# Lo parts of w_up by accumulating transfers in a two-layer hybrid encoder trunk

## The chip, the cores and the metric

The kernel runs on one core of one Trainium2 chip. The metric is the device time of one execution in microseconds. Other cores of the chip do no work of this kernel.

## The reference

The reference is a trunk of two layers over 256 tokens of width 2048, in float32. Each layer normalises the residual, projects it once, runs three groups of attention heads on the result, projects their concatenation back into the residual, and then applies an MLP with a squared ReLU:

```python
for l in range(DEPTH):                       # DEPTH = 2
    h = rmsnorm(x, norm_mix[l])
    proj = jnp.einsum('bsd,de->bse', h, w_in[l])          # 2048 x 3840
    ...                                                   # attention groups A, B, C
    x = x + jnp.einsum('bse,ed->bsd', mix, w_o[l])        # 2048 x 2048
    h = rmsnorm(x, norm_mlp[l])
    u = jax.nn.relu(jnp.einsum('bsd,df->bsf', h, w_up[l]))    # 2048 x 8192
    x = x + jnp.einsum('bsf,fd->bsd', u * u, w_down[l])       # 8192 x 2048
return rmsnorm(x, norm_final)
```

The change concerns the product with `w_up`, half of the MLP in each layer.

## The kernel before

**Two parts of a float32.** Every dense product is made on TensorE in three passes over operands of type fp32r. A weight tile W and an operand H are each split into a hi part, which is the value rounded to fp32r, and a lo part, which is the remainder W - hi. The three passes are hi·hi, hi·lo and lo·hi. Activations are split where they are made; weights are split as they arrive from memory.

**Steps.** The dense work is a list of 696 steps. A step takes one weight tile of 512 KB (128 partitions of 4 KB) and issues 24 matmuls with 256 columns (`w_up`, lines 611 to 613), or 12 with 512 columns (the other products, lines 446 to 448; one chunk of `w_in` has 24 of 256). A layer has 60 steps for `w_in`, 32 for `w_o`, and then the MLP in eight groups g: `up_steps(g)` has 16 steps (two chunks of 8), `down_steps(g)` has 16. They are listed as up(0), up(1), down(0), up(2), down(1), and so on to up(7), down(6), down(7). So in each layer the up steps come as one run of 32 and then six runs of 16, with 16 down steps between two runs; there are 128 up steps in a layer and 256 in all.

**Loading and splitting.** `load(i)` issues one transfer from the queue of SP into a tile `wraw` (six buffers). `split(i)` casts the tile to `whi` on ScalarE (line 783) and subtracts on VectorE to get `wlo` (line 784); `whi` and `wlo` have four buffers each. The loop over steps at the end issues loads up to 7 steps ahead (`LOOK_LOAD`) and splits up to 2 steps ahead (`LOOK_SPLIT`) of the step whose matmuls are written next. After each step `tick()` may add one piece of other work (attention, transposes). A scheduler then orders the instructions of each engine; each engine runs its own list in order.

**End of a chunk of w_up.** After the eighth step of a chunk, ScalarE applies ReLU to each of two PSUM banks (line 617), GpSimd squares the result in place (line 618), ScalarE casts it to hi (line 621) and VectorE subtracts for lo (line 622). These squares are all that GpSimd does in the up and down steps, except for the final norm.

Of the kernel before, what the change touches and what calls it, by code (L numbers as in the profile page):

```python
"""Hybrid encoder trunk (three attention groups, squared-ReLU MLP) on one core.

Dense products run on the tensor engine as float32 split exactly into two fp32r
parts (hi + lo); hi*hi + hi*lo + lo*hi carries float32's accuracy in three passes.
The residual stream, attention and normalisations stay on chip; only weights stream.
"""
# [27 lines left out]
OUT_ORDER = "ACB"  # L34
# mixer feature blocks of 256 (two k-blocks each): A 0-1, B 2-3, C 4-7
GROUP_BLOCKS = {"A": (0, 1), "B": (2, 3), "C": (4, 5, 6, 7)}
# [7 lines left out]
def tile_trunk(ctx: ExitStack, tc: tile.TileContext, x_in, w_in, w_o, w_up, w_down,  # L44
               gains, rowp, t5, rpb, gfin, cst, onehot, out):
    nc = tc.nc
    LOOK_LOAD, LOOK_SPLIT, BUDGET = 7, 2, 2.2
    N_WARM = 6
# [29 lines left out]

# [1 line left out]
    ident = cp.tile([P, P], F32, name="ident")  # L80
# [25 lines left out]
    def setup_tables():  # L106
        """Rope tables with the gains folded in: out = x * ctab + swap16(x) * stab."""
        nc.vector.tensor_scalar(negsink, rp[:, :, 0:8], -1.0, None, op0=ALU.mult)
        for l in range(L):
            nc.vector.tensor_scalar(rp[:, l, 8:72], rp[:, l, 8:72], 0.125, None, op0=ALU.mult)  # L110
            for which, off in (("q", 8), ("k", 72)):
                g = rp[:, l:l + 1, off:off + 64]
                c = cp.tile([P, NT, 64], F32, name=f"ctab_{which}{l}")
                s = cp.tile([P, NT, 64], F32, name=f"stab_{which}{l}")
                nc.vector.tensor_mul(c, cos_t, g.to_broadcast([P, NT, 64]))
                for a in range(4):
                    b = a ^ 1
                    nc.vector.tensor_mul(s[:, :, 16 * a:16 * a + 16], sin_t[:, :, 16 * a:16 * a + 16],
                                         g[:, :, 16 * b:16 * b + 16].to_broadcast([P, NT, 16]))
                ctab[which, l], stab[which, l] = c, s  # L120

    def setup_avec():
        """Relative-position vector of group A, reversed: avec[h, i] = bias(h, rel = 255 - i)."""
        t5x = cp.tile([33, 8], F32, name="t5x")
        nc.vector.memset(t5x[32:33, :], NEG)
        nc.sync.dma_start(t5x[0:32, :], t5)
        oh = dp.tile([33, 512], F32, tag="mid", bufs=6, name="oh")
        nc.sync.dma_start(oh, onehot)
        avs = dp.tile([8, 512], F32, tag="mid", bufs=6, name="avs")

        def mm():
            avp = tr_bank()
            nc.tensor.matmul(avp[0:8, :], t5x, oh, start=True, stop=True)
            nc.vector.tensor_copy(avs, avp[0:8, :])
            nc.sync.dma_start(avec, avs)
        add(mm, cost=0.9, delay=15.0)

# [1 line left out]
    bgq = []  # L139
# [7 lines left out]
    def add(fn, cost, after=(), delay=0):  # L147
        """Queue fn, `cost` us of PE time; it may start `delay` us from now or after the pieces in `after`."""
        p = Piece()
        p.fn, p.cost, p.after, p.delay, p.at, p.done = fn, cost, after, delay, cur[0], None  # L150
        bgq.append(p)
        return p
# [23 lines left out]

# [1 line left out]
    def hprep(key, gcol, j, hT, ss, done, fin_rs, late=0):  # L178
        """Column chunk j of x: partial sums of squares; k-blocks 4j..4j+3 of the operand."""
        def sq():  # L180
# [56 lines left out]

# [1 line left out]
    def q_transposes(src, pr0, qT):  # L239
        """src [P, t, heads*64]; 4 heads from pair pr0 -> qT [hi;lo, 4, 256]."""  # L240
        ps = tr_bank()
        psv = ps.rearrange("p (k t c) -> p k t c", k=2, t=NT)
        for pr in range(2):
            for t in range(NT):
                nc.tensor.transpose(psv[:, pr, t, :], src[:, t, (pr0 + pr) * P:(pr0 + pr + 1) * P], ident)  # L245
        psr = ps.rearrange("p (k c) -> p k c", k=2)
        for par in range(2):
            lo, hi = 64 * par, 64 * par + 64
            nc.scalar.copy(qT[0:64, par::2, :], psr[lo:hi, :, :])
        for par in range(2):  # L250
            lo, hi = 64 * par, 64 * par + 64
            nc.vector.tensor_sub(qT[64:128, par::2, :], psr[lo:hi, :, :], f(qT[0:64, par::2, :]))  # L252

    def k_transposes(src, pr0, npr, kh, kl):
        """src [P, t, heads*64]; head pairs pr0.. -> hi/lo [every head in both halves, heads, 256]."""
        ps = tr_bank()
        psv = ps.rearrange("p (k t c) -> p k t c", k=2, t=NT)
        for pr in range(npr):
            for t in range(NT):
                nc.tensor.transpose(psv[:, pr, t, :], src[:, t, (pr0 + pr) * P:(pr0 + pr + 1) * P], ident)  # L260
        psr = ps.rearrange("p (k c) -> p k c", k=2)[:, 0:npr, :]
        parts = [(slice(64 * half, 64 * half + 64), psr[64 * par:64 * par + 64], par)
                 for par in range(2) for half in range(2)]
        for rows, z, par in parts:
            nc.scalar.copy(kh[rows, par::2, :], z)
        for rows, z, par in parts:
            nc.vector.tensor_sub(kl[rows, par::2, :], z, f(kh[rows, par::2, :]))

    def v_split(ps, parts, t, r):
        """Value columns of one bank, scaled, as hi/lo; parts: (first column, heads, tile)."""  # L270
        src = [ps[:, c0:c0 + nh * 64].rearrange("p (h d) -> p h d", h=nh) for c0, nh, _ in parts]
# [6 lines left out]
    def rope(raw, H, which, l, outs):  # L278
        """raw [P, t, H, 64]: per-head RMS norm, gain and axial rotary, in place of outs(t)."""
        n = NT * H  # L280
# [21 lines left out]

# [1 line left out]
    class Unit:  # L304
# [4 lines left out]
    def queue_unit(u, *preps):  # L309
        """Scores, transposes of the weights, product with the values; spaced for the softmax between."""  # L310
        after = list(preps) + last_s[-1:]
# [86 lines left out]
    def mix_prep(l, grp, blk, raw, mixT, sqacc, done):  # L398
        """A finished block of 256 features: gained hi/lo operand and sum of squares."""
        m = big(F32R, 2, 2, 256)  # L400
# [30 lines left out]

# [1 line left out]
    steps = []  # L433

    class Step:
        def __init__(self, src, kk, n, pre, mm):
            self.src, self.kk, self.n, self.pre, self.mm = src, kk, n, pre, mm

    def mode_b(banks, h_tile, wh, wl, sub, first, last, n=512, blocks=(0, 1)):
        """out[tok, n] += operand^T W over the tile's k-blocks."""  # L440
        for t in blocks:
# [10 lines left out]
    def layer_steps(l):  # L452
# [10 lines left out]

        # -- input projection --
        def proj_evac(name, banks):
# [93 lines left out]

        # -- output projection --  # L560
        st["hT2"], st["ss2"] = [None] * 8, small(8)
# [26 lines left out]

        # -- MLP --
        uT = {}  # L590

        def up_steps(g):
            for c in range(2):
                fc = 2 * g + c
                box = {}
                for k in range(8):
# [3 lines left out]
                    def mm(wh, wl, k=k, fc=fc, box=box):  # L600
# [13 lines left out]
                        if k == 7:  # L614
                            for b in range(2):
# [7 lines left out]
                                uT[2 * fc + b] = u  # L623
                    steps.append(Step(w_up[l, fc * 8 + k], 2, 512, pre, mm))

# [48 lines left out]
    def final_chunk(j):  # L674
        """Squares of a finished column chunk; the final gain goes in ahead of the scale."""
        if not fin:
# [14 lines left out]
    def final_block(t):  # L691
        """Last chunk of token block t: norm over the whole row, scale, store."""
        square(3, t)
# [12 lines left out]

# [1 line left out]
    def bias_a(kv):  # L708
# [57 lines left out]

# [1 line left out]
    raw_t, hi_t, lo_t = {}, {}, {}  # L768

    def load(i):  # L770
        s = steps[i]
        w = wp.tile([P, s.kk, s.n], F32, tag="wraw", bufs=6, name=nm("wraw"))
        nc.sync.dma_start(w, s.src.rearrange("p (k n) -> p k n", k=s.kk))
        raw_t[i] = w

    def split(i):
        s = steps[i]
        w = raw_t.pop(i)
        h = wp.tile([P, s.kk, s.n], F32R, tag="whi", bufs=4, name=nm("whi"))
        lo = wp.tile([P, s.kk, s.n], F32R, tag="wlo", bufs=4, name=nm("wlo"))  # L780
        for part in ([slice(0, 1), slice(1, 2)] if i < 1 else [slice(0, s.kk)]):
            with tc.issue_after(h_act[-1]) if i < 2 else nullcontext():
                last_hi[0] = nc.scalar.copy(h[:, part], w[:, part]).ins  # L783
            nc.vector.tensor_sub(lo[:, part], w[:, part], f(h[:, part]))  # L784
        hi_t[i], lo_t[i] = h, lo

# [92 lines left out]
def _pack(w, nk):  # L879
    """[K, n] -> tiles [K/(128 nk), 128, nk*n]."""  # L880
    K, n = w.shape
# [61 lines left out]
```

## Time and profile before

| what | value |
|---|---|
| median of the two timed runs | 2089.51 us (2088.35 to 2090.66) |
| span of the profiled execution, first to last instruction | 2088.3 us |
| mean granted TensorE clock | 0.997 |
| TensorE busy with matmuls | 2066.0 us, 99% of the span |
| VectorE busy | 1273.8 us, 61% |
| ScalarE busy | 1041.4 us, 50% |
| GpSimd busy | 340.1 us, 16% |
| read from device memory | 377.34 MB |

The profiled execution has no time of its own beside its span; the lower of the two timed runs, 2088.35 us, is that span to within 0.1 us, so nothing measurable lies around it. "Busy" means that the engine had at least one instruction under way; matmuls overlap, so the busy time of TensorE doesn't say at what rate it worked. PE is TensorE's matmuls, PEld its weight loads, DVE VectorE, ACT ScalarE, POOL GpSimd and SP the engine that issues the loads. A window "A:B" is a stretch of the span in microseconds from its start.

### The profile page before, as it was taken

What the parts mean: (1) busy time and instruction counts of PE and PEld (TensorE: products, weight loads), DVE (VectorE), ACT (ScalarE), POOL (GpSimd) and SP (SyncE); (2) the same over time, 40 slices, a digit from 0 to 9 for tenths busy, and PEclk for the clock granted to TensorE, in tenths of its full rate; (3) what the DMA queues carried; (4) which work ended last, traced back from release to release, by engine and by line L of the source; (5) the groups of instructions that cost most, each with busy time, mean ns of one, the idle gap of its engine ahead of it and who ended that gap; (6) DMA issues with size and microseconds to landing.
All of it is one profiled execution on the core that took longest, in us unless ns stands there. A gap on an engine that the chain in (4) does not pass through costs nothing.

```text
span 2088.3 us, 31322 instructions
## 1 busy us (share of the span) xinstructions
PE 2066.0 (99%) x12444; PEld 1847.9 (88%) x12444; DVE 1273.8 (61%) x1426; ACT 1041.4 (50%) x1472; POOL 340.1 (16%) x362
## 2 busy tenths in 40 slices
PE   9999999999999999999999999999999999999998
PEld 7878889989899898998888788899899898999986
DVE  6777976454555545555668789754555545555555
ACT  6657755444344444434556566554344444434444
POOL 0484420000000000000005844101000000000001
PEclk9999999999999999999999999999999999999999
DMA  8545455565655656556556453555655656565563
GB/s 289 179 160 157 155 185 176 183 192 180 194 186 187 192 183 192 187 188 189 188 177 188 141 170 130 180 174 181 194 188 183 192 189 191 184 192 185 190 212 121
DMA packets 107550, 381.49 MB, mean 183 GB/s; under 512 B 11875, under 2 KB 14691, under 8 KB 107404
## 3 DMA queue, kind: packets, MB, share of 16 engines
q1 hardware_dynamic: 107116, 378.45, 56.6%
q8 instruction: 97, 1.59, 0.3%
q10 hardware_dynamic: 288, 1.05, 0.1%
q14 instruction: 49, 0.40, 0.1%
HBM read 377.34 MB, written 2.11 MB: 182 GB/s over the span
## 4 chain that ended last, share of the span: by engine, by line
PE 94%; POOL 2%; DVE 1%; ACT 1%; issue 1%; DMA 0%; SPq 0%; POOLq 0%; DVEq 0%
PE mm L446 18%; PE mm L447 18%; PE mm L448 18%; PE mm L612 12%; PE mm L613 12%; PE mm L611 12%; PE tr L362 1%; PE tr L192 1%; PE tr L381 1%; PE S L323 1%; PE S L322 1%; POOL big L300 1%; POOL big L506 0%; PE tr L245 0%; POOL sm L235 0%
## 5 line engine op out<-in xcount | busy, mean ns | idle before, releaser
L784 DVE TENSOR_TENSOR wlo<-wraw,whi 128x1024 fp32r<-128x1024 f32 (+1 forms) x697 | 863.4, 1241 | 697.4 <-ACT whi L783 695.0
L783 ACT CAST whi<-wraw 128x1024 fp32r<-128x1024 f32 (+1 forms) x697 | 729.9, 1048 | 884.6 <-PE mm L448 473.0
L446 PE MATMUL mm<-whi,big 128*128 128x512 f32 (+1 forms) x1792 | 695.7, 389 | 3.1 <-DVE big L252 3.1
L447 PE MATMUL mm<-wlo,big 128*128 128x512 f32 (+1 forms) x1792 | 693.0, 387 | 0.0
L448 PE MATMUL mm<-whi,big 128*128 128x512 f32 (+1 forms) x1792 | 692.4, 386 | 0.0
L611 PE MATMUL mm<-big,whi 128*128 128x256 f32 x2048 | 579.8, 283 | 0.0
L613 PE MATMUL mm<-big,wlo 128*128 128x256 f32 x2048 | 579.6, 283 | 0.0
L612 PE MATMUL mm<-big,whi 128*128 128x256 f32 x2048 | 579.6, 283 | 0.0
L446 PEld LDWEIGHTS mm<-whi,big 128*128 128x128 f32 x1792 | 337.8, 189 | 68.1 <-issue 3.4
L448 PEld LDWEIGHTS mm<-whi,big 128*128 128x128 f32 x1792 | 337.4, 188 | 68.0
L447 PEld LDWEIGHTS mm<-wlo,big 128*128 128x128 f32 x1792 | 337.9, 189 | 64.8 <-DVE wlo L784 0.2
L612 PEld LDWEIGHTS mm<-big,whi 128*128 128x128 f32 x2048 | 393.2, 192 | 0.5
L611 PEld LDWEIGHTS mm<-big,whi 128*128 128x128 f32 x2048 | 393.1, 192 | 0.5
L613 PEld LDWEIGHTS mm<-big,wlo 128*128 128x128 f32 x2048 | 393.1, 192 | 0.0
L618 POOL TENSOR_TENSOR mid<-mid 128x512 f32<-128x512 f32 x64 | 74.2, 1159 | 1247.3 <-ACT mid L617 1247.3
L353 POOL TENSOR_SCALAR big<-big,sm 128x256 f32<-128x256 f32 x128 | 87.5, 701 | 230.3 <-DVE sm L351 164.3
L643 DVE SCALAR_TENSOR_TENSOR x<-mm,sm,x 128x512 f32<-128x512 f32 x128 | 89.9, 744 | 4.5 <-PE mm L448 4.5
L622 DVE TENSOR_TENSOR big<-mid,big 128x512 fp32r<-128x512 f32 x64 | 44.1, 689 | 50.7 <-ACT big L621 50.7
L621 ACT CAST big<-mid 128x512 fp32r<-128x512 f32 x64 | 39.8, 621 | 50.7 <-POOL mid L618 50.7
L617 ACT ACTIVATE mid<-mm,zero 128x512 f32<-128x512 f32 x64 | 43.8, 684 | 39.5 <-PE mm L613 39.5
L235 POOL TENSOR_TENSOR sm<-sm,mhalf 128x2 f32<-128x2 f32 (+3 forms) x16 | 24.7, 1547 | 131.0 <-DVE sm L230 117.0
L364 DVE TENSOR_TENSOR big<-tr,big 128x512 fp32r<-128x512 f32 x64 | 41.1, 680 | 0.3
(117 smaller groups left out, 1013.2 us busy)
## 6 DMA issues: line engine op xcount, KB each, us to landing
wraw<-in_w_up_dram SPq DMA_DIRECT2D x256, 512.0 KB, 4.3
wraw<-in_w_down_dram SPq DMA_DIRECT2D x256, 512.0 KB, 4.1
wraw<-in_w_in_dram SPq DMA_DIRECT2D x120, 512.0 KB, 3.3
wraw<-in_w_o_dram SPq DMA_DIRECT2D x64, 512.0 KB, 3.6
biasB<-in_rpb_dram SPq DMA_DIRECT2D x16, 349.5 KB, 6.2
biasA<-avec SPq DMA_DIRECT2D x4, 768.0 KB, 4.9
x<-in_x_dram SPq DMA_DIRECT2D x3, 512.0 KB, 9.1
big<-in_gfin_dram SPq DMA_DIRECT2D x2, 512.0 KB, 4.3
```

The lines of the kernel that those rows point to most:

```text
L353: nc.gpsimd.tensor_scalar(p[:, s, :], p[:, s, :], rs[:, s:s + 1], 1.0, op0=ALU.mult, op1=ALU.mult)
L446: nc.tensor.matmul(o, a_h, wh[:, i, :], start=first and i == 0, stop=False)
L447: nc.tensor.matmul(o, a_h, wl[:, i, :], start=False, stop=False)
L448: nc.tensor.matmul(o, a_l, wh[:, i, :], start=False, stop=last and i == len(sub) - 1)
L611: nc.tensor.matmul(o, sh, ht[:, 0, kk, :], start=s0, stop=False, skip_group_check=True)
L612: nc.tensor.matmul(o, sh, ht[:, 1, kk, :], start=False, stop=False, skip_group_check=True)
L613: nc.tensor.matmul(o, sl, ht[:, 0, kk, :], start=False, stop=s1, skip_group_check=True)
L618: nc.gpsimd.tensor_mul(a, a, a)
L622: nc.vector.tensor_sub(uf[:, 1, :], a, f(uf[:, 0, :]))
L643: nc.vector.scalar_tensor_tensor(xs, box["b"][t], st["r2"][:, t:t + 1], xs, op0=ALU.mult, op1=ALU.add)
L783: last_hi[0] = nc.scalar.copy(h[:, part], w[:, part]).ins
L784: nc.vector.tensor_sub(lo[:, part], w[:, part], f(h[:, part]))
```

## The change

For the steps of `w_up` alone, `split` no longer subtracts on VectorE. ScalarE writes `lo = -w`, rounded to fp32r, which is the negated hi part, and `hi = w`, rounded likewise. Then a transfer issued from the queue of GpSimd reads the same weight tile from device memory a second time and adds it onto `lo` in SBUF, which leaves w - hi there. The other weights are split as before. Splits run 4 steps ahead instead of 2; `wraw` has 4 buffers instead of 6, `whi` and `wlo` have 5 each instead of 4, so the memory used is the same. The rest of the diff takes comments out, which moves line numbers.

```diff
-    LOOK_LOAD, LOOK_SPLIT, BUDGET = 7, 2, 2.2
+    LOOK_LOAD, LOOK_SPLIT, BUDGET = 7, 4, 2.2
...
     class Step:
-        def __init__(self, src, kk, n, pre, mm):
-            self.src, self.kk, self.n, self.pre, self.mm = src, kk, n, pre, mm
+        def __init__(self, src, kk, n, pre, mm, acc=False):
+            self.src, self.kk, self.n, self.pre, self.mm, self.acc = src, kk, n, pre, mm, acc
...
-                    steps.append(Step(w_up[l, fc * 8 + k], 2, 512, pre, mm))
+                    steps.append(Step(w_up[l, fc * 8 + k], 2, 512, pre, mm, acc=True))
...
     def load(i):
         s = steps[i]
-        w = wp.tile([P, s.kk, s.n], F32, tag="wraw", bufs=6, name=nm("wraw"))
+        w = wp.tile([P, s.kk, s.n], F32, tag="wraw", bufs=4, name=nm("wraw"))
         nc.sync.dma_start(w, s.src.rearrange("p (k n) -> p k n", k=s.kk))
         raw_t[i] = w
 
     def split(i):
         s = steps[i]
         w = raw_t.pop(i)
-        h = wp.tile([P, s.kk, s.n], F32R, tag="whi", bufs=4, name=nm("whi"))
-        lo = wp.tile([P, s.kk, s.n], F32R, tag="wlo", bufs=4, name=nm("wlo"))
+        h = wp.tile([P, s.kk, s.n], F32R, tag="whi", bufs=5, name=nm("whi"))
+        lo = wp.tile([P, s.kk, s.n], F32R, tag="wlo", bufs=5, name=nm("wlo"))
+        hi_t[i], lo_t[i] = h, lo
+        if s.acc:
+            nc.scalar.activation(lo, w, AF.Copy, scale=-1.0)
+            last_hi[0] = nc.scalar.copy(h, w).ins
+            nc.gpsimd.dma_start(lo, s.src.rearrange("p (k n) -> p k n", k=s.kk), accum_op=ALU.add)
+            return
         for part in ([slice(0, 1), slice(1, 2)] if i < 1 else [slice(0, s.kk)]):
             with tc.issue_after(h_act[-1]) if i < 2 else nullcontext():
                 last_hi[0] = nc.scalar.copy(h[:, part], w[:, part]).ins
             nc.vector.tensor_sub(lo[:, part], w[:, part], f(h[:, part]))
-        hi_t[i], lo_t[i] = h, lo
```

In the changed kernel the ReLU, square and hi cast of a chunk's end are lines 619, 620 and 623; the negation of `w_up` is line 785, its hi cast line 786, the accumulating transfer line 787, and the split of the other weights is lines 791 and 792. The matmuls of an up step are lines 613 to 615.

ScalarE at the end of the third chunk of the first layer's run of 32, before the change. `mid` is the chunk's result, `mm` its two PSUM banks:

```order
L783 CAST whi_4106<-wraw_3942 128x1024
L783 CAST whi_4138<-wraw_3972 128x1024
L617 ACTIVATE mid_4092<-mm_3856,zero_85 128x512
L783 CAST whi_4168<-wraw_4002 128x1024
L621 CAST big_4095<-mid_4092 128x512
L617 ACTIVATE mid_4098<-mm_3857,zero_85 128x512
L621 CAST big_4101<-mid_4098 128x512
L783 CAST whi_4198<-wraw_4032 128x1024
```

The same place on ScalarE after the change:

```order
L786 CAST whi_4141<-wraw_4034 128x1024
L785 ACTIVATE wlo_4142<-wraw_4034 128x1024
L619 ACTIVATE mid_4127<-mm_3884,zero_85 128x512
L786 CAST whi_4174<-wraw_4065 128x1024
L619 ACTIVATE mid_4133<-mm_3885,zero_85 128x512
L623 CAST big_4130<-mid_4127 128x512
L785 ACTIVATE wlo_4175<-wraw_4065 128x1024
L623 CAST big_4136<-mid_4133 128x512
L785 ACTIVATE wlo_4206<-wraw_4096 128x1024
L786 CAST whi_4205<-wraw_4096 128x1024
```

Each weight tile of `w_up` now has two instructions on ScalarE, the cast and the negation, and one negation (`wlo_4175`) stands behind both ReLUs and the first hi cast of the chunk.

GpSimd at the same place, before:

```order
L618 TENSOR_TENSOR mid_3838<-mid_3838 128x512
L618 TENSOR_TENSOR mid_3844<-mid_3844 128x512
L618 TENSOR_TENSOR mid_4092<-mid_4092 128x512
L618 TENSOR_TENSOR mid_4098<-mid_4098 128x512
L618 TENSOR_TENSOR mid_4346<-mid_4346 128x512
```

and after:

```order
L787 DMA wlo_4099<-in_w_up_dram 128x1024
L787 DMA wlo_4142<-in_w_up_dram 128x1024
L620 TENSOR_TENSOR mid_4127<-mid_4127 128x512
L620 TENSOR_TENSOR mid_4133<-mid_4133 128x512
L787 DMA wlo_4175<-in_w_up_dram 128x1024
L787 DMA wlo_4206<-in_w_up_dram 128x1024
```

Between the two squares of one chunk and those of the next stand eight issues of accumulating transfers, where there was nothing. The matmuls of the MLP stand in the same order on TensorE as before.

## The prediction

> **What bounds the kernel now.** I read the page first: the busy times and the chain of work that ended last.
>
> ```profile
> PE 2066.0 (99%) x12444; PEld 1847.9 (88%) x12444; DVE 1273.8 (61%) x1426; ACT 1041.4 (50%) x1472; POOL 340.1 (16%) x362
> ...
> PE 94%; POOL 2%; DVE 1%; ACT 1%; issue 1%; DMA 0%; SPq 0%; POOLq 0%; DVEq 0%
> ```
>
> TensorE is busy for all but 2088.3 - 2066.0 = 22.3 us, and 94% of the chain lies on it. No other engine and no transfer holds a visible share of the end. So whatever the change takes off VectorE or puts on ScalarE counts only if TensorE starts to wait. The view of waits, for TensorE alone, says how little it waits for weights today:
>
> ```profile
> PE tr L245 <- POOL big L506: 5.6, 2, 2.8
> PE mm L446 <- DVE big L252: 3.1, 2, 1.5
> PE tr L192 <- DMA x<-in_x_dram: 2.9, 2, 1.8
> ```
>
> The columns are total us, times, and the longest. None is a wait of an up step's matmul for `wlo` or `whi`. The split keeps ahead of TensorE everywhere.
>
> Next I need the time of one step, since everything new must fit into it. ScalarE's timeline shows it, because each cast waits for a buffer that a step's matmuls free. Columns are start, us, engine, line, operands, and in brackets the idle time before it with its releaser.
>
> ```profile
> 568.63 1.05 ACT L783 CAST whi<-wraw 128x1024 fp32r<-128x1024 f32 x1 [1.83 <-PE mm L612]
> 571.51 1.05 ACT L783 CAST whi<-wraw 128x1024 fp32r<-128x1024 f32 x1 [1.83 <-PE mm L612]
> ...
> 576.67 0.69 ACT L617 ACTIVATE mid<-mm,zero 128x512 f32<-128x512 f32 x1 [1.23 <-PE mm L613]
> 577.27 1.05 ACT L783 CAST whi<-wraw 128x1024 fp32r<-128x1024 f32 x1
> 578.51 0.62 ACT L621 CAST big<-mid 128x512 fp32r<-128x512 f32 x1 [0.19 <-POOL mid L618]
> 579.04 0.68 ACT L617 ACTIVATE mid<-mm,zero 128x512 f32<-128x512 f32 x1
> 581.11 0.62 ACT L621 CAST big<-mid 128x512 fp32r<-128x512 f32 x1 [1.39 <-POOL mid L618]
> 581.64 1.05 ACT L783 CAST whi<-wraw 128x1024 fp32r<-128x1024 f32 x1
> ...
> 614.06 1.05 ACT L783 CAST whi<-wraw 128x1024 fp32r<-128x1024 f32 x1 [1.67 <-PE mm L448]
> 616.78 1.05 ACT L783 CAST whi<-wraw 128x1024 fp32r<-128x1024 f32 x1 [1.67 <-PE mm L448]
> ```
>
> An up step takes 571.51 - 568.63 = 2.88 us, a down step 616.78 - 614.06 = 2.72 us.
>
> Last, the transfers. First the DMA view of the window 10:20, where many loads are queued at once, then the row of a window inside a run of up steps (columns: stretch, length, PE, PEld, DVE, ACT, POOL, clock, DMA share, GB/s), then the page's row on the loads of `w_up` (count, size, median us to landing).
>
> ```profile
> DMA packets 1402, 4.16 MB, mean 416 GB/s; under 512 B 127, under 2 KB 131, under 8 KB 1402
> ...
> q1 hardware_dynamic: 1402, 4.16, 103.2%
> ```
>
> ```profile
> 560.00:600.00 40.00, 40.00 (x336) 40.00 (x335) 18.46 (x16) 17.28 (x19) 2.32 (x2) 1.00 0.57 185
> ```
>
> ```profile
> wraw<-in_w_up_dram SPq DMA_DIRECT2D x256, 512.0 KB, 4.3
> ```
>
> With full queues the 16 engines move 416 GB/s, so a tile of 524,288 bytes costs 1.26 us of them. In the up run they are busy for 0.57 x 40 = 22.8 us for 336/24 = 14 tiles, 1.63 us a tile. That is the same tile at a less dense rate. I take 1.26 as the price when the engines are short, and 1.63 as its upper bound.
>
> The Trainium skill, "DMA: Bandwidth & Descriptors", section "Where 436 GB/s comes from", says that between HBM and SBUF about 358 GB/s binds. The 416 GB/s above speak against it; by 358 a tile would cost an estimated 1.46 us, and the sum below would be (3 x 1.46 - 2.88) x 256 = 387 us in place of 230.
>
> **The change, part by part.**
>
> *VectorE loses 256 subtractions, ScalarE gains 256 negations.*
>
> ```profile
> L784 DVE TENSOR_TENSOR wlo<-wraw,whi 128x1024 fp32r<-128x1024 f32 (+1 forms) x697 | 863.4, 1241 | 697.4 <-ACT whi L783 695.0
> L783 ACT CAST whi<-wraw 128x1024 fp32r<-128x1024 f32 (+1 forms) x697 | 729.9, 1048 | 884.6 <-PE mm L448 473.0
> ```
>
> VectorE saves 256 x 1.24 = 318 us, ScalarE gets 256 x 1.05 = 268 us, taking a negation for a cast of the same shape. In the up window ScalarE is busy 17.28 of 40 us; 14 negations make it 32.0. It still fits. Neither is on TensorE's path, so both count 0. The cover is ScalarE's remaining 8 us per 40. If a negation took over 1.62 us, ScalarE would be full and each further 0.1 us would cost 26 us.
>
> *Lead.* Five buffers and splits four steps ahead let the cast of a tile start once the step five before it is done, 4 x 2.88 = 11.5 us ahead of its use. The chain is cast and negation (2.1 us), issue, transfer, and its landing. With the median landing of a plain load, 4.3 us, that makes 6.4 us. At a chunk's end the negation of one tile stands behind the ReLUs and casts, which last from 576.67 to 581.64: 5.0 + 1.05 + 4.3 = 10.3 us, still inside 11.5. So latency alone costs 0, with 1.2 us to spare at that one place in eight steps; a landing of 7 us there would cost 32 chunks x 1.5 = 48 us.
>
> *GpSimd's queue gets 256 issues.* The trace has no transfer issued there. The nearest row is an issue by SP, minimum, median and maximum in ns:
>
> ```profile
> L773 SPq DMA_DIRECT2D wraw<-in_w_up_dram x256: 327/328/331, 302.9 to 1966.4; - x128
> ```
>
> Each issue waits on GpSimd for its negation, with the next squares of a chunk queued behind it, and ScalarE's hi cast and VectorE's lo behind those. The negation ahead of the squares belongs to a tile four steps on and needs only the step before the chunk's last, so the squares shouldn't be held. GpSimd is busy 2.32 of 40 us in the up window. It becomes the bound only if an issue takes over (40 - 2.32)/14 = 2.7 us; from 0.33 to 2.7 us it costs 0, and I take 0.
>
> *Transfers.* This is the term that decides. Each up step now has a plain load, 1.26 us, and an accumulating transfer of the same 512 KB. The trace shows none of that kind. Its lower bound is a plain load, one pass, 1.26 us: then 2.52 us fit into 2.88. But an accumulate must fetch the weight from device memory, fetch the old `lo` from SBUF, and write the sum. A plain load fetches once and writes once. If fetches set the pace, it costs two passes, 2.52 us; if fetch, fetch and write follow each other without overlap at the looser rate, 3 x 1.63 = 4.89 us. I take two passes, nearest to the full-queue row, since these engines will have full queues.
>
> The Trainium skill, "Collectives: The Full Stack", section "The bandwidth ceiling: the fold count and why AG ≠ RS ≠ AR", says that an add inside the DMA engines isn't slow for its arithmetic but because it reads two sources through the same ring, and gives 62.28 against 32.35 GB/s. By that ratio, 1.93, the accumulate would be an estimated 2.43 us and the sum 207 us; no run here shows it yet.
>
> Sum for a step: 1.26 + 2.52 = 3.78 us of the DMA engines against 2.88 us of TensorE, 0.90 us short, over 256 steps 230 us. What can be worked off ahead is little. In the four down steps ahead of a run the engines have 4 x (2.72 - 1.26) = 5.8 us to spare, so 14 runs could save at most 82 us. Against that stand tiles for the down steps that are loaded inside the run, and gaps in the engines' work when ScalarE pauses at a chunk's end. I count these as even and keep 230; with the whole credit it is about 150.
>
> *The rest.* Fewer `wraw` buffers with earlier splits keep the loads 7 steps ahead: 4 raw and 4 split in place of 6 and 2. The order of the attention pieces moves by a few instructions. I take 0, and ±10 us.
>
> The profiled execution: 2088.3 + 230 = 2318 us; its span is the lower of the timed runs and 1.2 us under their median, so 2320 us.
>
> **Rivals.**
>
> *Hidden transfers (not slower).* The accumulate costs one pass or a little more. For it: the transfer engines are busy only 0.57 of the up window, and the SBUF fetch could overlap the other. It decides at 2.88 - 1.26 = 1.62 us: below that the time is 2088 + 0 = 2090 us. Against it: the second fetch of the same bytes has to pass the same 16 engines.
>
> *A slower accumulate.* No overlap of the three accesses: at the dense rate 3 x 1.26 + 1.26 = 5.04 us a step, (5.04 - 2.88) x 256 = 553 us, 2640 us in all; at the loose rate 4.89 + 1.63 = 6.52, 932 us, 3020 us.
>
> *GpSimd's queue as the bound.* At 4 us an issue, (4 - 2.7) x 256 = 333 us, 2420 us. Against it: the 0.33 us of SP's issue, though those are made by another engine.
>
> *Faster.* TensorE's whole idle time is 22.3 us, 1.1%, and the up steps have none. A gain over 2% isn't there to be had.
>
> **How the numbers follow.** A measurement of this kernel tells 2%, 42 us, from no change. Chances: two passes 0.48 (own range 2235 to 2605: from the full credit, 2088 + 148, to all three passes of a step at the loose 1.63, (4.89 - 2.88) x 256 = 515); hidden 0.24; slower accumulate 0.18; GpSimd's queue 0.09; faster 0.01. All but the hidden case and the faster one are slower by over 2%: 0.75, with 0.24 within it. The range begins at the hidden case, 2085, since that alone holds more than may be left out, and ends at 2640, the three dense passes; looser ones are left out.
>
> **What would show it.** Right: TensorE waits in lines 613 to 615 for the DMA into `wlo`, some 0.9 us per up step; the up windows show a DMA share near 1.0 and the down windows 0.6 as now; busy time of PE falls to about 89% of the span. The accumulating transfers land in over 5 us. Hidden: PE stays at 99%, the DMA share in up windows is 0.85 to 0.95, and the waits for `wlo` are absent. A queue-bound GpSimd: the DMA share stays under 0.9 while TensorE waits, and GpSimd issues one transfer right after the other. What would make me wrong is the price of an accumulate alone: each 0.1 us of it above 1.62 us is 26 us of time.

## The result, and the profile after

The changed kernel takes 2297.75 us (2297.2 to 2298.3) against 2089.51 us before: a ratio of 1.0997, with a 95% interval of 1.0976 to 1.1018. The span of its profiled execution is 2296.5 us, 208.2 us above the 2088.3 us before. The time of that execution is 2298.3 us, so 1.8 us lie outside its span. The 0.1 us named for the kernel before doesn't show that, since its profiled execution has no time of its own. The forecast was 2320 us, with two passes of the transfer engines per accumulate as its mechanism.

The page of the kernel after, busy times, queues and the chain that ended last:

```profile
PE 2120.7 (92%) x12444; PEld 1858.9 (81%) x12444; DVE 970.5 (42%) x1170; ACT 1283.7 (56%) x1728; POOL 558.5 (24%) x618
...
q1 hardware_dynamic: 107116, 378.45, 47.9%
q0 software_dynamic: 36864, 134.23, 29.6%
...
PE 50%; DMA 35%; ACT 6%; issue 4%; POOL 3%; DVE 1%; ACTq 0%; SPq 0%; POOLq 0%; DVEq 0%
```

Before, 94% of the chain lay on TensorE and none on transfers; now transfers hold 35%, 27 of it on the plain loads of `w_up` and 8 on the accumulates. VectorE lost 303 us and ScalarE gained 242 us of busy time, and neither shows in the end. There is a new queue, q0, which carries the accumulating transfers.

Where TensorE waits now, matmuls and then weight loads (total us, times, longest):

```profile
PE mm L615 <- DMA wlo<-in_w_up_dram: 150.0, 209, 2.0
```

```profile
PEld mm L615 <- DMA wlo<-in_w_up_dram: 193.3, 213, 2.2
```

Line 615 is the third of an up step's three matmul lines, the one that reads `wlo`. Its wait stood in no row of before. The two rows are the same stalls, seen by the weight load and by the matmul behind it.

The DMA view of the window 360:400, inside the first run of up steps:

```profile
DMA packets 3016, 10.97 MB, mean 274 GB/s; under 512 B 346, under 2 KB 346, under 8 KB 3013
...
q0 software_dynamic: 1506, 5.46, 68.4%
q1 hardware_dynamic: 1507, 5.46, 36.4%
```

This is the central reading. The columns of the queues are packets, MB, and the time that the packets took as a share of all 16 engines' time; the shares can add up to a little over 100%. In the same 40 us both queues moved the same 5.46 MB, but the accumulating queue held the engines 68.4/36.4 = 1.88 times as long as the plain one. Together they move 274 GB/s of weights, so one plain and one accumulating tile take 2 x 524,288 / 274,000 = 3.83 us. The same stretch as a row of windows, for TensorE:

```profile
360.00:400.00 40.00, 33.25 (x256) 31.03 (x255) 3.69 (x4) 25.13 (x29) 12.14 (x14) 1.00 1.05 274
```

256 matmuls in 40 us are 10.7 steps of 3.75 us, where the run of before had 336 matmuls. The count takes in steps that the window cuts. TensorE's own rows give the step itself, since each step in here waits once for its tile:

```profile
381.65 0.39 PE L615 MATMUL mm<-big,wlo 128*128 128x256 f32 x1 [0.63 <-DMA wlo<-in_w_up_dram]
385.50 0.39 PE L615 MATMUL mm<-big,wlo 128*128 128x256 f32 x1 [0.70 <-DMA wlo<-in_w_up_dram]
389.27 0.39 PE L615 MATMUL mm<-big,wlo 128*128 128x256 f32 x1 [0.64 <-DMA wlo<-in_w_up_dram]
...
404.50 0.39 PE L615 MATMUL mm<-big,wlo 128*128 128x256 f32 x1 [0.64 <-DMA wlo<-in_w_up_dram]
```

From 381.65 to 404.50 are six steps, 3.81 us each. The landing times of the page complete it:

```profile
wraw<-in_w_up_dram SPq DMA_DIRECT2D x256, 512.0 KB, 11.8
wlo<-in_w_up_dram POOLq DMA_DIRECT2D x256, 512.0 KB, 12.3
wraw<-in_w_down_dram SPq DMA_DIRECT2D x256, 512.0 KB, 4.3
```

The plain loads of `w_up` land as late as the accumulates, as they would if both queue for the same engines; those of `w_down` land about as before.

### The profile page after: what moved, and what is told of

The parts are those of the page before. It is cut to its first block, busy times and chain, and to the rows that moved or that the text cites. A ratio compares the mean times of both kernels' runs of the same rounds, so it can differ in the third digit from the quotient of the medians.

```text
span 2296.5 us, 31991 instructions
## 1 busy us (share of the span) xinstructions
PE 2120.7 (92%) x12444; PEld 1858.9 (81%) x12444; DVE 970.5 (42%) x1170; ACT 1283.7 (56%) x1728; POOL 558.5 (24%) x618
## 3 DMA queue, kind: packets, MB, share of 16 engines
q0 software_dynamic: 36864, 134.23, 29.6%
q8 instruction: 97, 1.59, 0.3%
q10 hardware_dynamic: 288, 1.05, 0.1%
HBM read 511.56 MB, written 2.11 MB: 224 GB/s over the span
## 4 chain that ended last, share of the span: by engine, by line
PE 50%; DMA 35%; ACT 6%; issue 4%; POOL 3%; DVE 1%; ACTq 0%; SPq 0%; POOLq 0%; DVEq 0%
DMA wraw<-in_w_up_dram 27%; PE mm L448 15%; PE mm L449 15%; PE mm L450 15%; DMA wlo<-in_w_up_dram 8%; ACT wlo L785 3%; ACT whi L786 1%; PE tr L362 1%; PE mm L615 1%; PE tr L381 1%; PE mm L614 1%; PE mm L613 1%; PE S L323 1%; PE S L322 1%; POOL big L353 1%
## 5 line engine op out<-in xcount | busy, mean ns | idle before, releaser
L792 DVE TENSOR_TENSOR wlo<-wraw,whi 128x1024 fp32r<-128x1024 f32 (+1 forms) x441 | 548.4, 1248 | 563.8 <-ACT whi L791 562.3
L791 ACT CAST whi<-wraw 128x1024 fp32r<-128x1024 f32 (+1 forms) x441 | 462.2, 1050 | 573.5 <-PE mm L450 361.2
L615 PE MATMUL mm<-big,wlo 128*128 128x256 f32 x2048 | 602.3, 294 | 150.1 <-DMA wlo<-in_w_up_dram 150.0
L787 POOL DMA_DIRECT2D wlo<-in_w_up_dram x256 | 222.2, 868 | 987.7 <-ACT wlo L785 926.1
L786 ACT CAST whi<-wraw 128x1024 fp32r<-128x1024 f32 x256 | 267.3, 1045 | 273.1 <-DMA wraw<-in_w_up_dram 241.1
L785 ACT ACTIVATE wlo<-wraw 128x1024 fp32r<-128x1024 f32 x256 | 271.1, 1059 | 58.7 <-PE mm L449 54.0
L624 DVE TENSOR_TENSOR big<-mid,big 128x512 fp32r<-128x512 f32 x64 | 52.5, 820 | 562.8 <-ACT big L623 562.8
## 6 DMA issues: line engine op xcount, KB each, us to landing
wlo<-in_w_up_dram POOLq DMA_DIRECT2D x256, 512.0 KB, 12.3
```

The source lines that it names most:

```text
L615: nc.tensor.matmul(o, sl, ht[:, 0, kk, :], start=False, stop=s1, skip_group_check=True)
L785: nc.scalar.activation(lo, w, AF.Copy, scale=-1.0)
L786: last_hi[0] = nc.scalar.copy(h, w).ins
L787: nc.gpsimd.dma_start(lo, s.src.rearrange("p (k n) -> p k n", k=s.kk), accum_op=ALU.add)
```

## The experiments

My theory after the result: the transfer engines set the pace in up steps, because an accumulate holds them for about two passes. Against it stood four others: a landing of 12 us is longer than the lead of 11.5 us that the buffers give; GpSimd's queue or ScalarE's negations are too slow; device memory can't be read that fast; or each accumulate costs a fixed sum wherever it stands. The first experiment was timed ten times, the others once each. The runs of the kernel before beside them lie between 2088.18 and 2091.77 us, so a difference of a few us says little.

**Everything but the transfer.**

```diff
-            nc.gpsimd.dma_start(lo, s.src.rearrange("p (k n) -> p k n", k=s.kk), accum_op=ALU.add)
+            nc.vector.tensor_add(lo, f(lo), w)
```

> Everything of the change but the transfer: ScalarE negates and casts, the buffers and the splits four steps ahead stay, and VectorE adds the raw tile onto the negated hi part (256 additions of 1.24 us) in place of the accumulating transfer. Two passes on the transfer engines (my theory): the loss is all in the transfer, so 2090 us, within 15 us of the kernel before. ScalarE, the lead or the buffers as the cause: it stays near 2298 us.

Measured: 2090.99 us, a ratio to before of 1.0004 (0.9994 to 1.0013). ScalarE carries the negations in the up steps, 30.99 of 40 us against the forecast 32.0:

```profile
360.00:400.00 40.00, 40.00 (x336) 40.00 (x335) 18.48 (x16) 30.99 (x34) 2.56 (x3) 1.00 0.58 192
```

So negations, other buffers and earlier splits together cost nothing that shows. The whole loss is in the transfer.

**The same transfer without the addition.**

```diff
-            nc.gpsimd.dma_start(lo, s.src.rearrange("p (k n) -> p k n", k=s.kk), accum_op=ALU.add)
+            nc.gpsimd.dma_start(lo, s.src.rearrange("p (k n) -> p k n", k=s.kk))
```

> The same transfer from GpSimd's queue without the addition: the weight tile overwrites the negated hi part, so lo is the whole weight. Same bytes from device memory, same queue, same waits. Two passes: without the second fetch it costs 1.3 to 1.4 us of the engines, 2.8 us a step with the plain load against 2.88, so 2090 to 2120 us. Read volume of device memory or GpSimd's queue as the cause: 2298 us.

Measured: 2091.57 us. Windows row and DMA view of 360:400:

```profile
360.00:400.00 40.00, 40.00 (x336) 40.00 (x335) 1.88 (x2) 30.54 (x34) 10.14 (x17) 1.00 1.03 367
```

```profile
DMA packets 4014, 14.66 MB, mean 367 GB/s; under 512 B 442, under 2 KB 442, under 8 KB 4011
...
q0 software_dynamic: 2011, 7.32, 51.7%
q1 hardware_dynamic: 2000, 7.30, 51.4%
```

The same bytes are read from device memory a second time, from the same queue and with the same waits, and TensorE doesn't lose a microsecond: 336 matmuls in 40 us, 367 GB/s, both queues with the same share for the same bytes. So it isn't GpSimd's queue that makes a transfer dear, nor the second read of the weights. The addition, with all that belongs to it, is what costs. Note the share of 1.03: the engines read as full here as in the kernel after, yet they keep up. A share of 1.0 alone is therefore no proof of a bound; the waits of TensorE and the rate are.

**Accumulates without the plain loads.** ScalarE splits one tile that is loaded once, in place of each tile of `w_up`; `lo` then holds the weight less the rounded fixed tile.

```diff
+    fixed = []
...
         s = steps[i]
-        w = wp.tile([P, s.kk, s.n], F32, tag="wraw", bufs=4, name=nm("wraw"))
+        if s.acc:
+            if not fixed:
+                fixed.append(cp.tile([P, 2, 512], F32, name="wfix"))
+                nc.sync.dma_start(fixed[0], s.src.rearrange("p (k n) -> p k n", k=s.kk))
+            raw_t[i] = fixed[0]
+            return
+        w = wp.tile([P, s.kk, s.n], F32, tag="wraw", bufs=3, name=nm("wraw"))
```

> Accumulating transfers stay, the plain loads of w_up go (ScalarE splits one fixed tile instead, so lo is the difference of two different tiles). Three raw buffers. Two passes: 2.6 us of the engines a step against 2.88, hidden, 2090 to 2100 us with a DMA share of about 0.9 in up windows. A long landing of each accumulate, whatever else the engines do, or GpSimd's queue as the bound: 2298 us.

Measured: 2095.67 us, 5 us above before. Of these, 3 lie ahead of the first up step (331.0 us against 327.9), and TensorE waits for an accumulate once, 0.4 us. The accumulates alone fit:

```profile
360.00:400.00 40.00, 40.00 (x336) 40.00 (x335) 1.88 (x2) 30.52 (x33) 14.27 (x16) 1.00 1.02 186
```

All 256 accumulates are issued by GpSimd, at the pace of TensorE, and now land in a median of 5.6 us. So neither GpSimd's queue nor a long landing of its own makes the loss; the 12.3 us of the kernel after come only with the plain loads beside them. The DMA share was 1.02 where I expected 0.9.

**The source in SBUF.** The transfer adds the raw tile from SBUF, so `w_up` is read once; the raw tile is held until the transfer has landed, which needs other buffers.

```diff
-            nc.gpsimd.dma_start(lo, s.src.rearrange("p (k n) -> p k n", k=s.kk), accum_op=ALU.add)
+            nc.gpsimd.dma_start(lo, w, accum_op=ALU.add)
...
-    LOOK_LOAD, LOOK_SPLIT, BUDGET = 7, 4, 2.2
+    LOOK_LOAD, LOOK_SPLIT, BUDGET = 7, 3, 2.2
...
-        w = wp.tile([P, s.kk, s.n], F32, tag="wraw", bufs=4, name=nm("wraw"))
+        w = wp.tile([P, s.kk, s.n], F32, tag="wraw", bufs=6, name=nm("wraw"))
...
-        h = wp.tile([P, s.kk, s.n], F32R, tag="whi", bufs=5, name=nm("whi"))
-        lo = wp.tile([P, s.kk, s.n], F32R, tag="wlo", bufs=5, name=nm("wlo"))
+        h = wp.tile([P, s.kk, s.n], F32R, tag="whi", bufs=4, name=nm("whi"))
+        lo = wp.tile([P, s.kk, s.n], F32R, tag="wlo", bufs=4, name=nm("wlo"))
```

> The accumulating transfer takes its source from the raw tile in SBUF in place of device memory, so that w_up is read once. Six raw buffers, four of whi and wlo, splits three steps ahead (a raw tile is now held until the transfer has landed). Two passes: both fetches and the write stay, so 2280 to 2330 us. Device memory as the bound: 2090 to 2110 us.

Measured: 2306.12 us. Device memory gives 377.34 MB as before in place of 511.56, and the loss stays. DMA view of 360:400:

```profile
DMA packets 3018, 10.99 MB, mean 275 GB/s; under 512 B 343, under 2 KB 343, under 8 KB 3015
...
q0 software_dynamic: 1494, 5.42, 69.1%
q1 hardware_dynamic: 1521, 5.53, 35.8%
```

These are the numbers of the kernel after to within two per cent. It doesn't matter here where the addend comes from, so device memory isn't the bound.

**Half and three quarters of the tiles.**

```diff
-                    steps.append(Step(w_up[l, fc * 8 + k], 2, 512, pre, mm, acc=True))
+                    steps.append(Step(w_up[l, fc * 8 + k], 2, 512, pre, mm, acc=k % 2 == 0))
```

> Every other tile of w_up by an accumulating transfer, the others split on VectorE. Two passes: 1.26 + 2.57/2 = 2.55 us of the engines a step on average, below 2.88, so 2090 to 2105 us. A landing longer than the lead as the cause: still at least half of the 208 us, 2190 us or more.

The other kernel of the pair has `acc=k % 4 != 3` there.

> Three of four tiles of w_up by an accumulating transfer. Two passes: 1.26 + 0.75 x 2.57 = 3.19 us a step, 0.31 us short, 79 us over 256 steps less some 35 us worked off ahead, so 2125 to 2170 us. A cost that goes with the number of transfers: 2089 + 0.75 x 208 = 2245 us.

Measured: 2096.05 us and 2166.84 us, with 2089.91 us before on the same chip, so 6 and 77 us. The loss isn't in proportion to the number of transfers: half of them cost 6 us, the next quarter 71, the last 131. It sets in between a sum of 2.55 us for a step and one of 3.19 us, and TensorE's 2.88 us lie between them, as for a limit of throughput. A fixed sum for each transfer would have cost 104 and 156 us. One thing doesn't fit: at three quarters the sum gave 79 us, less some 35 us worked off ahead, and 77 us were lost. That credit doesn't show there, and why wasn't traced.

**Tiles of w_down too.**

```diff
-                    steps.append(Step(w_down[l, (g * 4 + j) * 4 + k], 2, 512, None, mm))
+                    steps.append(Step(w_down[l, (g * 4 + j) * 4 + k], 2, 512, None, mm, acc=True))
```

> All tiles of w_down by accumulating transfers as well, 512 in all, so that the engines have no easy steps to recover in. Two passes: 512 steps of 3.83 us in place of 256 of 2.88 and 256 of 2.72, that is 2088 + 1961 - 1434 = 2615 us, DMA share 1.0 through the whole MLP. A cost that goes with the number of transfers: 2089 + 2 x 208 = 2506 us.

Measured: 2617.75 us, 3 us from the sum and 112 us above a cost in proportion to the number. DMA view of 700:900, up and down steps mixed:

```profile
DMA packets 15059, 54.93 MB, mean 275 GB/s; under 512 B 1672, under 2 KB 1672, under 8 KB 15048
...
q0 software_dynamic: 7515, 27.36, 68.6%
q1 hardware_dynamic: 7533, 27.43, 36.5%
```

The pace is the same over 200 us whatever TensorE does with the tiles, with a step of 2 x 524,288 / 275,000 = 3.81 us.

**Less lead.** As the kernel after, with the look-ahead and the buffers of the SBUF experiment's diff (three steps ahead, six raw, four of `whi` and `wlo`).

> As after, but splits three steps ahead, six raw buffers and four of whi and wlo. Two passes: the engines set the pace whatever the lead, 2290 to 2325 us. Lead as the cause (a landing of 12 us spread over the buffers): 3.83 x 5/4 = 4.79 us a step, 2298 + 256 x 0.96 = 2540 us.

Measured: 2340.3 us, 15 us above the end of what I expected from two passes and 200 us short of the lead theory. The rate inside the run is unchanged (278 GB/s in 360:400), so the lead isn't the bound there, but it does something. ScalarE's first ReLU of a run's last chunk shows what: it waits for TensorE, and so marks TensorE's pace. The two rows of each kernel belong to the run of 32 and the next run of 16, one cycle of 16 down and 16 up steps apart. Kernel before, after and shallow, in this order:

```profile
420.47 0.69 ACT L617 ACTIVATE mid<-mm,zero 128x512 f32<-128x512 f32 x1 [1.23 <-PE mm L613]
...
510.09 0.69 ACT L617 ACTIVATE mid<-mm,zero 128x512 f32<-128x512 f32 x1 [1.23 <-PE mm L613]
```

```profile
449.30 0.69 ACT L619 ACTIVATE mid<-mm,zero 128x512 f32<-128x512 f32 x1 [0.95 <-PE mm L615]
...
551.32 0.69 ACT L619 ACTIVATE mid<-mm,zero 128x512 f32<-128x512 f32 x1 [0.93 <-PE mm L615]
```

```profile
449.54 0.69 ACT L619 ACTIVATE mid<-mm,zero 128x512 f32<-128x512 f32 x1 [2.19 <-PE mm L615]
...
554.70 0.69 ACT L619 ACTIVATE mid<-mm,zero 128x512 f32<-128x512 f32 x1 [2.09 <-PE mm L615]
```

A cycle takes 89.6 us before, 102.0 after, 105.2 with less lead. Sixteen steps that are 0.95 us short make 15.2 us; the kernel after loses 12.4. So 2.8 us a run are worked off ahead, about one accumulate, and with one step less of lead nothing is (105.2 - 89.6 = 15.6 us are lost). That led to two runs with more lead.

**More lead, two raw buffers.**

```diff
-    LOOK_LOAD, LOOK_SPLIT, BUDGET = 7, 4, 2.2
+    LOOK_LOAD, LOOK_SPLIT, BUDGET = 7, 5, 2.2
...
-        w = wp.tile([P, s.kk, s.n], F32, tag="wraw", bufs=4, name=nm("wraw"))
+        w = wp.tile([P, s.kk, s.n], F32, tag="wraw", bufs=2, name=nm("wraw"))
...
-        h = wp.tile([P, s.kk, s.n], F32R, tag="whi", bufs=5, name=nm("whi"))
-        lo = wp.tile([P, s.kk, s.n], F32R, tag="wlo", bufs=5, name=nm("wlo"))
+        h = wp.tile([P, s.kk, s.n], F32R, tag="whi", bufs=6, name=nm("whi"))
+        lo = wp.tile([P, s.kk, s.n], F32R, tag="wlo", bufs=6, name=nm("wlo"))
```

> As after, but splits five steps ahead, two raw buffers and six of whi and wlo: the reverse of the shallow kernel. If the engines set the pace inside a run and the splits' lead only says how many accumulating transfers are done ahead of a run, one more tile of 2.6 us is done ahead of each of 14 runs: 2298 - 36 = 2262 us, while 8 up steps inside a run still take 30.5 us. If two raw buffers starve the splits, it is slower than after, 2300 us or more, and ScalarE waits for raw tiles in the down steps too. If the lead were the bound inside a run, 2298 - 256 x 0.64 = 2134 us.

Measured: 2645.62 us. This says nothing on the lead, since the two raw buffers starve everything, as the second case of the expectation had it:

```profile
ACT wlo L785 <- DMA wraw<-in_w_up_dram: 561.3, 229, 6.7
ACT whi L791 <- DMA wraw<-in_w_down_dram: 419.7, 207, 5.4
```

**More lead, four raw buffers.**

```diff
-    LOOK_LOAD, LOOK_SPLIT, BUDGET = 7, 4, 2.2
+    LOOK_LOAD, LOOK_SPLIT, BUDGET = 8, 5, 2.2
...
-        return dp.tile([P, *shape], dt, tag="big", bufs=24, name=nm("big"))
+        return dp.tile([P, *shape], dt, tag="big", bufs=22, name=nm("big"))
...
-        h = wp.tile([P, s.kk, s.n], F32R, tag="whi", bufs=5, name=nm("whi"))
-        lo = wp.tile([P, s.kk, s.n], F32R, tag="wlo", bufs=5, name=nm("wlo"))
+        h = wp.tile([P, s.kk, s.n], F32R, tag="whi", bufs=6, name=nm("whi"))
+        lo = wp.tile([P, s.kk, s.n], F32R, tag="wlo", bufs=6, name=nm("wlo"))
```

> The deep kernel without starving the raw tiles: splits five and loads up to seven steps ahead, four raw buffers as in after, six of whi and wlo, paid for by two of the 24 buffers of activations. If the lead only says how many accumulating transfers are done ahead of a run: a cycle of 16 up and 16 down steps takes 102.0 - 2.6 = 99.4 us and 8 up steps inside a run still 30.3 to 30.6 us, so 2298 - 36 = 2262 us, plus what the missing activation buffers cost in the attention part, which the first up step's time shows. If the lead bound the steps inside a run: 8 up steps in 25 to 26 us, 2140 us or less.

Measured: 2258.07 us. Two of TensorE's waits inside the run of 32, eight steps apart, and then the same rows of ScalarE's timeline:

```profile
410.26 0.39 PE L615 MATMUL mm<-big,wlo 128*128 128x256 f32 x1 [0.73 <-DMA wlo<-in_w_up_dram]
...
440.84 0.39 PE L615 MATMUL mm<-big,wlo 128*128 128x256 f32 x1 [0.73 <-DMA wlo<-in_w_up_dram]
```

```profile
443.08 0.68 ACT L619 ACTIVATE mid<-mm,zero 128x512 f32<-128x512 f32 x1
...
542.58 0.68 ACT L619 ACTIVATE mid<-mm,zero 128x512 f32<-128x512 f32 x1
```

Eight steps inside the run of 32 take 440.84 - 410.26 = 30.6 us, 3.82 us each, as in the kernel after; a cycle takes 99.5 us against the forecast 99.4. (These two ReLUs follow another instruction of ScalarE without a wait, so the cycle is good to some tenths of a us.) With one more pair of buffers and both look-aheads raised by one, some 2.5 us more are worked off ahead in a cycle, about one accumulate, and 40 us in all; inside a run nothing changes. The expectation names seven steps for the loads, and the kernel has eight. The missing activation buffers cost nothing ahead of the MLP: the first up step starts at 327.6 us, and at 329.8 us in the kernel after.

One difference stays open: the kernel with the source in SBUF is 34 us faster than the shallow one, which has the same buffers and look-ahead (2306.12 against 2340.3 us). Its rate inside a run is the same. The traces show where it gains. At the first run of 16 its first two steps go at 2.88 us, while in the shallow kernel TensorE waits in the first step already. In the 12 us from the first accumulate ahead of that run on (488:500, and 487:499 in the shallow kernel), the queues of the first moved 1.58 MB of accumulates beside 1.32 MB of plain loads, and those of the shallow kernel 1.34 beside 1.59. A raw tile that is held until its transfer has landed leaves fewer loads to run ahead, which fits; that it is the cause wasn't tried.

No version made here beats the kernel before; TensorE is idle for 22.3 us of that span, and removing waits can't gain more.

## Why the prediction was right

**The deciding term.** I took two passes for the accumulate, 3.78 us a step with the plain load. Measured: 3.83 us a step by the rate of 274 GB/s and 3.81 us by TensorE's rows, with 1.88 times the engine time for the accumulate. The shortfall is 0.95 us a step in place of 0.90. Three passes of 524,288 bytes in 3.83 us are 411 GB/s, near the 416 GB/s from which I took the price of a pass; the looser 1.63 us of the up window would have been wrong, and the run without the addition moved 367 GB/s through the same engines. That an accumulate takes about two passes is shown. That the second one is the fetch of the old `lo` was my reason for it, and no run here separates that fetch from the addition itself.

The Trainium skill, "Collectives: The Full Stack", section "The bandwidth ceiling: the fold count and why AG ≠ RS ≠ AR", gives a ratio of 1.93 between a collective that copies and one that adds. This case's trace agrees with its 1.88. The estimate of 207 us from that ratio lies beside the measured 208 by luck: it makes a step 3.69 us, where 3.83 was measured, and it leaves out what is worked off ahead. The same skill, "DMA: Bandwidth & Descriptors", section "Where 436 GB/s comes from", lets about 358 GB/s bind between HBM and SBUF. The trace of before has 416 GB/s, and the estimate of 387 us from the lower rate, a step of 4.39 us, is refuted.

**The step that was mis-sized.** I set what is worked off ahead of a run, at most 82 us, against tiles loaded early and gaps, and counted nothing. Summed over the 14 runs, from the first to the last matmul of each, TensorE takes 206 us longer than before (12.2 to 14.6 us for a run of 16, 27 us for one of 32), and the first up step starts 1.9 us later, at 329.8 us: together the 208 us. Against 256 x 0.95 = 243 us that is a credit of 37 us, 2.6 a run. The credit was less than 82 us because the lead set it, and not the slack of the down steps: it moved with one step more or less of lead. That the forecast came within 22 us is in part luck, since the two errors have opposite signs: the step was 0.05 us too short, 13 us in all, and the credit that was left out is 37 us.

**The terms at zero.** VectorE, ScalarE and the rest were each put at 0; the run without the transfer shows them together at 0.2 us between the medians, within -1.3 to +2.7 by its interval. It says nothing on the lead or on GpSimd's issues, which belong to the transfer. An issue takes longer than the 0.33 us of SP, though far under the 2.7 us from which it would decide:

```profile
L787 POOL DMA_DIRECT2D wlo<-in_w_up_dram x256: 853/866/1066, 317.7 to 2185.7; - x128
```

The lead of 11.5 us turned out shorter than the landing of 12.3 us, which I hadn't foreseen. That landing goes with the pressed engines and isn't the cause: it is 5.6 us without the plain loads, and with more or less lead the pace inside a run stays.

**The rivals.** Hidden transfers were refuted by the price alone, about 2.57 us (3.83 less 1.26) against the threshold of 1.62 us. Half of the tiles by accumulate, where the sum stays under 2.88 us, cost 6 us, which agrees with that threshold but doesn't measure it. Three accesses one after the other would have cost 553 us. GpSimd's queue was cleared by the run without plain loads and by the one without the addition.

**What I said would show it.** The waits in line 615 came as said, as did the DMA share near 1.0 in up windows (1.05) and near 0.6 in down windows (0.62 in 460:485, which holds down steps alone), and landings of over 5 us (12.3). The busy time of TensorE fell to 92% of the span, where I said 89%. Of the 208 us, 153.5 are idle time and 54.7 are busy time. In the rows above, the matmul behind a wait takes 0.39 us where the mean was 0.283 before, and it overlaps with none before it, as matmuls otherwise do; so each wait also lengthens the busy time. That is why the waits view has 150 us, 0.59 us a step, and not 0.9. For hidden transfers I named a DMA share of 0.85 to 0.95; the hidden cases showed 1.00 (half of the tiles) to 1.03, so that sign would have misled.

## What to carry to other kernels

In this kernel an accumulating transfer costs the transfer engines about twice a plain one of the same bytes, whether its addend lies in device memory or in SBUF. Before moving an elementwise operation from an engine with time to spare into the transfers, add up the engines' microseconds for one step of the loop and compare with the step. Buffers and look-ahead here only moved work from one phase into the slack of the one before, as long as there were enough raw buffers; inside a long phase they didn't change the pace.

## What the runs showed of the hardware

- The bytes of the new queue count the addend once: 134.23 MB for 256 tiles. What the addition takes beyond a plain write appears only in the packets' time, 68.4% against 36.4% in 360:400.
- The share of DMA time reads 1.0 before TensorE has to wait for them: 1.02 at 186 GB/s with accumulates alone, 1.03 at 367 GB/s with two plain streams, each with TensorE unhindered, and 1.05 at 274 GB/s where it waits.
- GpSimd needs 866 ns for the issue of an accumulating transfer of this shape, 537 ns for a plain one (the run without the addition), SP 328 ns for a plain one.
- In the run with two raw buffers TensorE's waits reach 6.8 us and the mean granted clock falls to 0.941; the kernel before had 0.998 on the same chip. With waits of at most 2.0 us, in the kernel after, it is 0.996, and with up to 3.4 us, in the run with less lead, 0.997.
